# A two-layer encoder trunk: the first weight sums of the second MLP matrices, formed by GpSimd

## The chip, the core and the metric

One core of a Trainium2 chip runs the whole program. Its engines work in parallel, each through its own queue in order: TensorE multiplies, VectorE, ScalarE and GpSimd do element-wise work, SyncE (SP) issues most of the DMAs; GpSimd issues the DMAs that add into on-chip memory. The metric is the device time of one execution in microseconds (us); lower is better.

## The reference

A mixer layer with causal forgetting attention and a second one with chunked attention, each followed by a squared-ReLU MLP, on 256 tokens of width 2048 in float32. The change touches only the MLPs:

```python
D_MODEL = 2048; SEQ = 256; DEPTH = 2; D_FF = 4 * D_MODEL

def rms_norm(x, g):
    xf = x.astype(jnp.float32)
    y = xf * lax.rsqrt(jnp.mean(xf * xf, axis=-1, keepdims=True) + EPS)
    return (y * g.astype(jnp.float32)).astype(x.dtype)

def sq_relu_mlp(h, g, w1, w2):
    a = jax.nn.relu(rms_norm(h, g) @ w1)
    return (a * a) @ w2
...
        h = h + sq_relu_mlp(h, mlp_norm_g[layer], mlp_w1[layer], mlp_w2[layer])
```

## The kernel before

**Products.** The activations stay on the chip as the stationary operand; the weights stream through TensorE once, 512 columns at a time, for two blocks of 128 tokens. To keep float32 accuracy on a faster matmul type, every operand is split into a rounded part `hi` and a remainder `lo`, and each product takes three passes: hi x hi (line 491), lo of the activations x hi of the weights (493), hi x lo of the weights (495). For every weight tile ScalarE makes `hi` (line 227) and VectorE makes `lo`, a subtraction of two on-chip tiles (line 228). There are three `hi` and three `lo` buffers, filled ahead of TensorE by `top_up`.

**Pairs.** In the MLPs two 512-column output panels form a pair. Part of each pair is computed with seven products instead of eight block products (a Strassen-like scheme): the weight blocks are "11", "12", "21", "22", and the products take the tiles "11", T3 = 22 + 12, T2 = T3 + 11, T1 = 12 + 11, "21", T4 = 21 + T2 and "22", in this order (class `Form`). The rest of the pair's weights goes through as plain units of 128 x 1024 (`raw`). An MLP works in four chunks of 2048 hidden columns; each chunk has two pairs for its part of the first matrix and then two for the second matrix. The pairs of the second matrix are "deep" (`p.deep`): their blocks are 2048 columns wide and their forms are used in two halves of 1024 columns. There are 4 x 2 deep pairs in a layer, 16 in all. Below, the first and the second pair mean the two deep pairs of one chunk.

**Who makes the sums.** T3 and T2 are additions in `make` (line 848), T2 in the place of T3 (the tile is named `wT`); T1 and T4 are made by `put` (line 854), a DMA from GpSimd's queue that adds a block from memory to a tile on the chip: T1 to block "12" once T3 has read it, T4 to T2 once T2's `hi` and `lo` are made. `prepare(p, d)` starts the loads of the blocks (`bring`, line 832, SP's queue) and the sums when `d` plain units are left before the pair begins: for the second pair "12" at 7, "22" at 5, "21" at 1, "11" at 4, T3's first half at 3 and its second at 2, T1 at 2; for the first pair "12" at 8, "22" at 6, T3 at 4 and 3.

**Around them.** VectorE also makes `act` (line 882, the low part of the hidden activations), the activation sums of the scheme (lines 296 to 299, and their low part, line 306), transposes finished hidden panels from the accumulators into `z` (line 341), which go through DRAM (lines 351, 357) or directly (`hop`, line 367, eight of its DMAs from GpSimd's queue) to their turned place, and adds finished panels to the residual stream (line 613). The queues of VectorE, ScalarE, TensorE and SP run in the order in which the code is written (`keep_order`); GpSimd is not in that list.

Of the kernel before, what the change touches and what calls it, by code (L numbers as in the profile page):

```python
# [12 lines left out]
ALU = mybir.AluOpType  # L13
# [37 lines left out]
def trunk(ctx: ExitStack, tc: tile.TileContext, xT, xr, gs, hg, bf, wgate, w_in, w_oa, w1a, w1fa, w1sa, w2fa, w2sa,  # L51
          w_kv, w_qb, w_ob, w1b, w1fb, w1sb, w2fb, w2sb, rel, out):
    nc = tc.nc
    V, S, G, TE, SY = nc.vector, nc.scalar, nc.gpsimd, nc.tensor, nc.sync
# [158 lines left out]
    def issue(parts=1):  # L213
        form = None
        if not raws:
            load(parts)
        raw, cuts = raws.popleft()
        if not cuts:
            form, half = raw, raw.half
            raw, cuts = form.pair.t[form.name], [slice(0, form.pair.cols - UN if half else UN)]  # L220
            if half:
                raw = raw[:, UN:]
        n = cuts[-1].stop
        hi = wsp.tile([P, n], F32R, name="hi" if n == UN else "hih", bufs=3 if n == UN else 1)
        lo = wsp.tile([P, n], F32R, name="lo" if n == UN else "loh", bufs=3 if n == UN else 1)
        for c in cuts:
            S.activation(hi[:, c], raw[:, c], AF.Copy)  # L227
            V.tensor_tensor(lo[:, c], raw[:, c], hi[:, c].bitcast(F32), op=ALU.subtract)  # L228
        ready.append((hi, lo, n < UN))
        if form and form.pair.deep and form.name == "T3":  # L230
            make(form.pair, "T2", int(half))
        elif form and half == form.pair.wide:
            if form.name == "T3":
                make(form.pair, "T2")
            elif form.name == "T2" and form.pair.adds:
                put(form.pair, "T4")
# [72 lines left out]
    def room(tag, name, dtype=F32):  # L309
        return qkv.tile([P, DEEP], dtype, name=name, tag=tag, bufs=1)  # L310
# [18 lines left out]
    def steps(make):  # L329
        box = []  # L330

        def step():
            if not box:
                box.append(make())
            next(box[0])
        return step
# [40 lines left out]
    def query_room(i):  # L377

        if not query:
            query.append(prob.tile([P, 4 * UN], F32, name="query", tag="p", bufs=1))  # L380
        return query[0][:, i * UN : i * UN + UN]
# [452 lines left out]
    def make(p, name, half=None):  # L834
        t = p.t
        if half == 1:
            pass
        elif name == "T3":
            if p.order in ("query", ""):
                t[name] = query_room(0)  # L840
            else:
                t[name] = prob.tile([P, 4 * UN], F32, name="wT3", tag="p", bufs=1) if p.order == "early" else room("bias", "wT3")
        else:
            t[name] = t[{"T1": "12", "T2": "T3", "T4": "11"}[name]]
        a, b = {"T1": ("12", "11"), "T3": ("22", "12"), "T2": ("T3", "11"), "T4": ("21", "T2")}[name]
        cols = slice(0, p.cols) if half is None else slice(half * UN, min(half * UN + UN, p.cols))
        d, a, b = (t[i][:, cols] for i in (name, a, b))
        V.tensor_tensor(d, a, b, op=ALU.add)  # L848

    def put(p, name):  # L850

# [262 lines left out]
```

## Time and profile before

| | us |
|---|---|
| median of 3 runs | 2094.65 |
| lowest, highest | 2094.32, 2102.31 |
| span of the profiled execution | 2090.4 |
| TensorE busy | 2076.3 |
| VectorE busy | 1679.5 |
| ScalarE busy | 1288.4 |
| GpSimd busy | 150.1 |

The profile is one execution; its span runs from the first to the last instruction on the engines, and no time of its own stands beside it other than that span. Rows of a timeline read: start, duration, engine, line, operation, output<-inputs, and in brackets the idle time of the engine before it with what ended it. "x2" means two instructions merged into one row. In a group's row, the numbers behind the bar are busy time in us and the mean of one in ns, then the idle time before.

### The profile page before, as it was taken

Reading aid. Unit: us, or ns where it says so; the run is one execution under the profiler, and the core shown is the slowest. Engines: PE = TensorE matmul, PEld = TensorE weight load, DVE = VectorE, ACT = ScalarE, POOL = GpSimd, SP = SyncE. Lnnn points to the kernel's source line nnn. Section 1 sums busy time; section 2 is a strip of 40 time slices with the busy share of each in tenths; the row PEclk is TensorE's granted clock in tenths of the full one; section 3 lists DMA queues with packets and bytes.
Section 4 is the critical chain, followed back from the end, with each engine's and each line's share of the span. In section 5 each row is a group of like instructions: output and inputs, shape, how many; then the busy total and the mean of one; then the engine's idle time right before and its main releaser. Section 6 shows DMA issues by size and latency. Waiting matters only on the chain.

```text
span 2090.4 us, 26489 instructions
## 1 busy us (share of the span) xinstructions
PE 2076.3 (99%) x9182; PEld 1709.6 (82%) x9182; DVE 1679.5 (80%) x1972; ACT 1288.4 (62%) x1613; POOL 150.1 (7%) x195
## 2 busy tenths in 40 slices
PE   9999999999999999999999999999999999999999
PEld 7888888878887887887878888888788788878877
DVE  5767666889789889889988577778988897898886
ACT  6544454767567667667776445556765675676674
POOL 1111000001001001001011001000010010010010
PEclk9999999999999999999999999999999999999999
DMA  7777778789689789788878777787987986897885
GB/s 285 248 253 240 232 255 264 250 268 296 232 292 283 241 270 298 231 273 287 280 252 269 233 232 234 247 264 266 294 280 233 284 284 232 291 286 237 274 279 182
DMA packets 176151, 545.14 MB, mean 261 GB/s; under 512 B 37760, under 2 KB 70416, under 8 KB 163728
## 3 DMA queue, kind: packets, MB, share of 16 engines
q1 hardware_dynamic: 163088, 477.31, 64.4%
q0 software_dynamic: 12640, 65.57, 16.2%
q8 instruction: 72, 1.18, 0.2%
q14 instruction: 63, 0.52, 0.1%
q10 hardware_dynamic: 288, 0.57, 0.1%
HBM read 503.49 MB, written 35.68 MB: 258 GB/s over the span
## 4 chain that ended last, share of the span: by engine, by line
PE 86%; DVE 5%; DMA 5%; ACT 2%; issue 2%; SPq 1%; ACTq 0%; DVEq 0%
PE acc L491 22%; PE acc L493 22%; PE acc L495 22%; PE s L495 6%; PE s L491 5%; PE s L493 5%; DVE lo L228 3%; DMA turn<-z 2%; DMA raw<-in_w1sa 1%; ACT hi L227 1%; PE s L635 1%; PE po L665 1%; DVE z L341 1%; DMA raw<-in_w1sb 1%; SPq L357 0%
## 5 line engine op out<-in xcount | busy, mean ns | idle before, releaser
L228 DVE TENSOR_TENSOR lo<-raw,hi 128x1024 fp32r<-128x1024 f32 (+1 forms) x542 | 655.2, 1214 | 189.3 <-ACT hi L227 176.1
L227 ACT ACTIVATE hi<-raw 128x1024 fp32r<-128x1024 f32 (+1 forms) x542 | 569.3, 1053 | 311.3 <-PE acc L493 232.4
L491 PE MATMUL acc<-hi,act 128*128 128x512 f32 x2092 | 580.4, 394 | 1.3 <-ACT hi L227 1.3
L495 PE MATMUL acc<-lo,act 128*128 128x512 f32 x2092 | 571.6, 390 | 0.0
L493 PE MATMUL acc<-hi,act 128*128 128x512 f32 x2092 | 571.0, 389 | 0.1
L493 PEld LDWEIGHTS acc<-hi,act 128*128 128x128 f32 x2092 | 392.7, 188 | 83.0 <-DVE act L321 0.7
L495 PEld LDWEIGHTS acc<-lo,act 128*128 128x128 f32 x2092 | 391.3, 188 | 84.6 <-DVE lo L228 3.4
L491 PEld LDWEIGHTS acc<-hi,act 128*128 128x128 f32 x2092 | 390.5, 188 | 82.0 <-ACT hi L227 3.2
L227 ACT ACTIVATE hi<-w 128x1024 fp32r<-128x1024 f32 x202 | 212.7, 1057 | 93.4 <-PE acc L493 42.9
L228 DVE TENSOR_TENSOR lo<-w,hi 128x1024 fp32r<-128x1024 f32 x202 | 245.5, 1219 | 22.4 <-ACT hi L227 19.1
L228 DVE TENSOR_TENSOR lo<-wT,hi 128x1024 fp32r<-128x1024 f32 x142 | 172.2, 1221 | 60.8 <-ACT hi L227 59.1
L227 ACT ACTIVATE hi<-wT 128x1024 fp32r<-128x1024 f32 x142 | 148.1, 1055 | 74.4 <-PE acc L493 32.2
L495 PE MATMUL s<-lo,act 128*128 128x512 f32 x370 | 102.1, 392 | 6.0 <-DVE lo L228 6.0
L491 PE MATMUL s<-hi,act 128*128 128x512 f32 x370 | 101.1, 390 | 0.0
L493 PE MATMUL s<-hi,act 128*128 128x512 f32 x370 | 100.9, 389 | 0.0
L495 PEld LDWEIGHTS s<-lo,act 128*128 128x128 f32 x370 | 68.7, 188 | 23.8 <-DVE lo L228 10.1
L493 PEld LDWEIGHTS s<-hi,act 128*128 128x128 f32 x370 | 69.5, 188 | 14.4
L491 PEld LDWEIGHTS s<-hi,act 128*128 128x128 f32 x370 | 69.3, 188 | 14.5 <-ACT hi L227 0.3
L848 DVE TENSOR_TENSOR wT<-wT,w 128x1024 f32<-128x1024 f32 (+1 forms) x48 | 66.3, 1381 | 1.6
L668 ACT ACTIVATE act<-po 128x256 fp32r<-128x256 f32 x32 | 12.3, 385 | 88.0 <-PE po L666 88.0
L848 DVE TENSOR_TENSOR wT<-w,w 128x1024 f32<-128x1024 f32 (+1 forms) x48 | 65.5, 1364 | 0.3 <-DMA w<-in_w2fa 0.3
L577 POOL TENSOR_TENSOR ss<-ss,mhalf 128x4 f32<-128x4 f32 x32 | 43.5, 1367 | 271.8 <-DVE ss L576 271.8
(209 smaller groups left out, 1968.8 us busy)
## 6 DMA issues: line engine op xcount, KB each, us to landing
raw<-in_w_in SPq DMA_DIRECT2D x95, 512.0 KB, 4.6
raw<-in_w1sa SPq DMA_DIRECT2D x70, 512.0 KB, 6.4
raw<-in_w1sb SPq DMA_DIRECT2D x70, 512.0 KB, 6.1
w<-in_w2fa SPq DMA_DIRECT2D x32, 1024.0 KB, 7.7
raw<-in_w2sa SPq DMA_DIRECT2D x64, 512.0 KB, 8.0
raw<-in_w_kv SPq DMA_DIRECT2D x64, 512.0 KB, 4.7
w<-in_w2fb SPq DMA_DIRECT2D x32, 1024.0 KB, 7.5
raw<-in_w2sb SPq DMA_DIRECT2D x64, 512.0 KB, 7.3
```

What stands on the lines that cost most here:

```text
L227: S.activation(hi[:, c], raw[:, c], AF.Copy)
L228: V.tensor_tensor(lo[:, c], raw[:, c], hi[:, c].bitcast(F32), op=ALU.subtract)
L341: V.transpose(z.rearrange("p (j n b c) -> p b n j c", j=4, n=n, b=nb)[:, b], src.rearrange("p (n j c) -> p n j c", n=n, j=4))
L491: TE.matmul(ps[:, cols], xh, cut(hi, j), start=first, stop=False, **kw)
L493: TE.matmul(ps[:, cols], xl, cut(hi, j), start=False, stop=False, **kw)
L495: TE.matmul(ps[:, cols], xh, cut(lo, j), start=False, stop=last, **kw)
L577: G.tensor_tensor(rn, vv, mhalf, op=ALU.pow)
L635: TE.matmul(s[:, P : 3 * P], q[:, a, P:T], k[:, a], start=True, stop=True)
L665: TE.matmul(po[:, :T], v[:, 0, a * P : (a + 1) * P], pT[:, :2], start=True, stop=False)
L668: S.activation(o[i][:, 0], po[:, :T], AF.Copy)
L848: V.tensor_tensor(d, a, b, op=ALU.add)
```

## The change

One line of `make`: in the deep pairs T3's two additions are issued on GpSimd (`G`) instead of VectorE (`V`). T2, and T3 of all other pairs, stay on VectorE.

```diff
         a, b = {"T1": ("12", "11"), "T3": ("22", "12"), "T2": ("T3", "11"), "T4": ("21", "T2")}[name]
         cols = slice(0, p.cols) if half is None else slice(half * UN, min(half * UN + UN, p.cols))
         d, a, b = (t[i][:, cols] for i in (name, a, b))
-        V.tensor_tensor(d, a, b, op=ALU.add)
+        (G if p.deep and name == "T3" else V).tensor_tensor(d, a, b, op=ALU.add)
```

VectorE's queue at a first pair of layer 2 (`wT_15437` is T3, `w_15352` block "22", `w_15270` block "12", `w_15435` block "11"):

```order
 L306 TENSOR_TENSOR Sh<-sum,Sh 128x512 x2
-L848 TENSOR_TENSOR wT_15437<-w_15352,w_15270 128x1024
-L228 TENSOR_TENSOR lo<-raw,hi 128x1024
-L882 TENSOR_TENSOR act<-q,act 128x1024
-L341 STREAM_TRANSPOSE z<-acc 128x4x4x32 x2
-L848 TENSOR_TENSOR wT_15437<-w_15352,w_15270 128x1024
+L228 TENSOR_TENSOR lo<-raw,hi 128x1024
+L882 TENSOR_TENSOR act<-q,act 128x1024
+L341 STREAM_TRANSPOSE z<-acc 128x4x4x32 x2
 L228 TENSOR_TENSOR lo<-w_15435,hi 128x1024
 L296 TENSOR_TENSOR sum<-q 128x256
```

The two additions leave the queue; what stood between and behind them keeps its order.

VectorE's queue at the second pair of the same chunk (`wT_15793` is its T3, `w_15748` its block "11"):

```order
 L228 TENSOR_TENSOR lo<-w_15352,hi 128x1024 x2
 L882 TENSOR_TENSOR act<-q,act 128x1024
-L848 TENSOR_TENSOR wT_15793<-w_15708,w_15605 128x1024
-L228 TENSOR_TENSOR lo<-raw,hi 128x1024 x2
-L228 TENSOR_TENSOR lo<-w_15748,hi 128x1024
-L848 TENSOR_TENSOR wT_15793<-w_15708,w_15605 128x1024
-L228 TENSOR_TENSOR lo<-w_15748,hi 128x1024
+L228 TENSOR_TENSOR lo<-raw,hi 128x1024 x2
+L228 TENSOR_TENSOR lo<-w_15748,hi 128x1024 x2
 L613 SCALAR_TENSOR_TENSOR h_90<-acc,qn,h_90 128x512
```

Here five `lo`, `act` and residual instructions close up where the two additions stood.

GpSimd's queue over both pairs (`w_15270` and `w_15605` become T1, `wT_15437` and `wT_15793` become T4 in the DMAs of line 854):

```order
 L854 DMA w_14968<-in_w1fb 128x1536
 L854 DMA wT_15099<-in_w1fb 128x1536
+L848 TENSOR_TENSOR wT_15437<-w_15352,w_15270 128x1024 x2
 L854 DMA w_15270<-in_w2fb 128x2048
 L854 DMA wT_15437<-in_w2fb 128x2048
 L367 DMA q<-z 32x256 x8
+L848 TENSOR_TENSOR wT_15793<-w_15708,w_15605 128x1024 x2
 L854 DMA w_15605<-in_w2fb 128x2048
 L854 DMA wT_15793<-in_w2fb 128x2048
```

The two additions of a pair stand next to each other, ahead of the pair's T1 and behind the DMAs of the pair before; those of the second pair also stand behind the eight DMAs of the hop.

## The prediction

> **What bounds the kernel now.** I read the page's busy table first, then who waited for whom on TensorE, then the stretches around the moved additions, and last the timelines of VectorE and TensorE there.
>
> ```profile
> span 2090.4 us, 26489 instructions
> PE 2076.3 (99%) x9182; PEld 1709.6 (82%) x9182; DVE 1679.5 (80%) x1972; ACT 1288.4 (62%) x1613; POOL 150.1 (7%) x195
> L495 PE MATMUL s<-lo,act 128*128 128x512 f32 x370 | 102.1, 392 | 6.0 <-DVE lo L228 6.0
> ```
> ```profile
> PEld s L495 <- DVE lo L228: 15.3, 19, 1.4
> PE s L495 <- DVE lo L228: 7.0, 10, 0.9
> ```
> ```profile
> 1819.00:1852.00 33.00, 32.40 (x139) 25.29 (x138) 30.55 (x35) 24.23 (x27) 4.03 (x7) 1.00 0.96 300
> 1852.00:1880.00 28.00, 28.00 (x125) 23.17 (x125) 25.28 (x24) 18.35 (x19) 2.57 (x5) 1.00 0.88 280
> ```
>
> TensorE (PE) is the bound. It is unoccupied for 2090.4 - 2076.3 = 14.1 us in all, and 7.0 us of that are ten waits of line 495, the pass that needs `lo` from VectorE (DVE); the weight loads show 19 such waits. A matmul is drawn 392 ns long, but four of them start in 0.91 us (1867.01 to 1867.92, quoted below), 0.227 us each, so every wait also hides up to 392 - 227 = 0.165 us. All that VectorE's lateness costs TensorE is therefore at most 7.0 + 19 x 0.165 = 10.1 us, 0.48%. No relief of VectorE can bring more. The two stretches are one first and one second pair of the second matrices (columns: length, then PE, PEld, DVE, ACT, POOL busy, clock, DMA share, GB/s). VectorE is busy 30.55 of 33 us and 25.28 of 28 us there: it has some 2.5 us to spare in each, and added VectorE time beyond that must reach TensorE.
>
> **The change, part by part.** It removes 32 additions from VectorE (16 pairs, two each).
>
> ```profile
> L848 DVE TENSOR_TENSOR wT<-w,w x48: 1181/1219/1752, 349.5 to 2035.3; 128x1024 f32<-128x1024 f32 x34, 128x1536 f32<-128x1536 f32 x14
> ```
>
> One takes 1.22 us, but back to back two start 1.14 us apart (1864.32 and 1865.45 below), so a pair gives VectorE 2 x 1.14 = 2.28 us of slots, 36.5 us in all.
>
> It adds two GpSimd (POOL) additions per pair. The trace has no such instruction; the nearest rows are its masks over one input and its small two-input powers, with the VectorE rows beside one power:
>
> ```profile
> L805 POOL TENSOR_SCALAR_AFFINE_SELECT nb<-nb 128x512 f32<-128x512 f32 x4 | 2.5, 634 | 0.0
> masks.py:199 POOL TENSOR_SCALAR_AFFINE_SELECT ident<-ident 128x128 f32<-128x128 f32 x1 | 0.3, 285 | 0.1
> L577 POOL TENSOR_TENSOR ss<-ss,mhalf x32: 1003/1114/1932, 48.0 to 1304.2; 128x4 f32<-128x4 f32 x32
> 1106.04 1.93 POOL L577 TENSOR_TENSOR ss<-ss,mhalf 128x4 f32<-128x4 f32 x1 [9.36 <-DVE ss L576]
> ```
> ```profile
> 1105.85 1.22 DVE L228 TENSOR_TENSOR lo<-query,hi 128x1024 fp32r<-128x1024 f32 x1
> 1106.99 1.22 DVE L228 TENSOR_TENSOR lo<-raw,hi 128x1024 fp32r<-128x1024 f32 x1
> ```
>
> Duration: a mask costs 634 ns for 512 columns and 285 ns for 128, that is 0.91 ns a column and 0.17 us fixed. If 1024 columns of two inputs ran like 1024 of one, the add takes 0.17 + 0.93 = 1.1 us: the lower end. If the inputs are read one after the other, 2048 columns: 0.17 + 1.86 = 2.03 us, or 4 x 634 ns = 2.54 us without splitting off the fixed part: the upper end. I take 2.3 us, between the last two, since the instruction has two inputs.
>
> By the Trainium skill, GPSIMD Engine Reference, section 3.1 (Elementwise — side-by-side cycle accounting), a GpSimd add of two 2048-column inputs takes 4497 ns; half of it, 2.25 us, is an estimate that would move the sum below by less than 2 us.
>
> Contention: a power takes 1.00 us at its shortest. The one at 1106.04 began while a subtraction of two on-chip inputs ran on VectorE (until 1105.85 + 1.22 = 1107.07) and took 1.93 us: 1.03 us of waiting and 0.90 us of work. So a GpSimd read waits for a VectorE instruction with two on-chip inputs, and is let in behind one instruction although the next already stood at 1106.99. Whether VectorE waits the other way round no row shows, as four columns are read in no time. The bounds: VectorE is not held at all, or for the whole 2.3 us. I take the whole, because a read path that makes one side wait for a full instruction is not divided column by column. Every `lo` subtraction (L228), `act` (L882), sum and second weight sum (L848) has two on-chip inputs; the transposes (L341) and the residual updates (L613), which read accumulators, have not.
>
> The Trainium skill, SBUF — State Buffer, section "Who interferes with whom", says just this: a VectorE instruction with two SBUF inputs contends with a GpSimd instruction that reads SBUF, and the later one fully blocks. The trace agrees for the one direction, with the 1.93 us; by that rule the sum is the one below.
>
> Place: on VectorE the second addition had a slot several instructions behind the first; on GpSimd they stand next to each other and start when block 22 has landed. No other operation stands in GpSimd's queue between the previous pair's DMA and them. T1's accumulating DMA behind them had to wait for both additions before, too, so it is not put behind anything new. First pair, layer 2:
>
> ```profile
> 1813.75 0.37 SPq L832 DMA_DIRECT2D w<-in_w2fb  x1
> 1818.28 0.42 SPq L832 DMA_DIRECT2D w<-in_w2fb  x1
> ```
> ```profile
> 1818.93 1.28 DVE L306 TENSOR_TENSOR Sh<-sum,Sh 128x512 fp32r<-128x512 f32 x2
> 1820.13 1.22 DVE L848 TENSOR_TENSOR wT<-w,w 128x1024 f32<-128x1024 f32 x1
> 1821.52 1.23 DVE L228 TENSOR_TENSOR lo<-raw,hi 128x1024 fp32r<-128x1024 f32 x1 [0.17 <-ACT hi L227]
> 1823.56 1.23 DVE L882 TENSOR_TENSOR act<-q,act 128x1024 fp32r<-128x1024 f32 x1 [0.81 <-ACT q L878]
> 1824.70 1.31 DVE L341 STREAM_TRANSPOSE z<-acc 128x512 f32<-128x512 f32 x2
> 1825.93 1.18 DVE L848 TENSOR_TENSOR wT<-w,w 128x1024 f32<-128x1024 f32 x1
> 1827.09 1.23 DVE L228 TENSOR_TENSOR lo<-w,hi 128x1024 fp32r<-128x1024 f32 x1
> 1829.70 1.22 DVE L228 TENSOR_TENSOR lo<-w,hi 128x1024 fp32r<-128x1024 f32 x1
> ```
> ```profile
> 1829.00 0.62 PE L495 MATMUL s<-lo,act 128*128 128x512 f32 x2
> 1830.97 0.73 PE L495 MATMUL s<-lo,act 128*128 128x512 f32 x2 [0.45 <-DVE lo L228]
> ```
>
> Block 22 was issued at 1813.75 and used at 1820.13 without a wait, so it was there by then; I let the first add start after the first half of L306, 1819.6 to 1821.9. L306's other half follows (to 1822.4), then the second add (to 1824.7), then `lo` 1824.7, L882 1825.9, the transposes 1827.0 to 1828.3. The `lo` of 1827.09 thus starts at 1828.3, ends at 1829.5, 0.5 us after TensorE wanted it (1829.00). The sums and the next `lo`, 2.61 us behind it in the rows, start 1.06 us later than 1829.70 once the last slack is used; at 1830.97 TensorE already stands waiting, so the whole 1.06 us is new: **+1.06 us per first pair**.
>
> Second pair, layer 2:
>
> ```profile
> 1863.17 1.23 DVE L882 TENSOR_TENSOR act<-q,act 128x1024 fp32r<-128x1024 f32 x1 [0.82 <-ACT q L878]
> 1864.32 1.22 DVE L848 TENSOR_TENSOR wT<-w,w 128x1024 f32<-128x1024 f32 x1
> 1865.45 2.35 DVE L228 TENSOR_TENSOR lo<-raw,hi 128x1024 fp32r<-128x1024 f32 x2
> 1868.86 1.22 DVE L848 TENSOR_TENSOR wT<-w,w 128x1024 f32<-128x1024 f32 x1
> 1869.99 1.22 DVE L228 TENSOR_TENSOR lo<-w,hi 128x1024 fp32r<-128x1024 f32 x1
> ```
> ```profile
> 1867.01 1.07 PE L495 MATMUL acc<-lo,act 128*128 128x512 f32 x4
> 1867.92 1.07 PE L491 MATMUL acc<-hi,act 128*128 128x512 f32 x4
> 1869.73 1.07 PE L495 MATMUL acc<-lo,act 128*128 128x512 f32 x4
> ```
>
> Add one 1864.3 to 1866.6, the first `lo` 1866.6 to 1867.8 (wanted at 1867.01: 0.8 us late), add two 1867.7 to 1870.0, the second `lo` 1870.0 to 1871.3 (wanted at 1869.73): **+1.6 us per second pair**. From there on the freed slot at 1868.86 brings VectorE back and nothing more is lost.
>
> Sum: 8 x 1.06 + 8 x 1.6 = 8.5 + 12.8 = **+21 us**. Against the profiled span 2090.4 us that is 2111.7; the median of the runs, 2094.65, lies 4.25 us above the span, and gives **2116 us**. With 1.8 us per add the same steps leave nothing at the first pairs and about 0.6 us at the second, +5 us; with 2.54 us, 1.5 and 2.1, +29 us.
>
> **Rivals.** (1) No blocking, or adds short enough to fit VectorE's spare time: not slower than before. For it: VectorE's rows show no held instruction anywhere; against it: the 1.93 us power. Little would be gained even so. The stalls of the first pairs begin at `lo` 1827.09, whose `hi` waits not for VectorE but for a weight block:
>
> ```profile
> 1826.00 2.01 ACT L227 ACTIVATE hi<-w 128x1024 fp32r<-128x1024 f32 x2 [2.47 <-DVE z L341]
> w<-in_w2fb SPq DMA_DIRECT2D x32, 1024.0 KB, 7.5
> ```
>
> The row names the transpose, but `hi` reads nothing of it; block 11, issued at 1818.28, lands a median 7.5 us later, at 1825.8. The removed addition leaves a hole there. I give this 2094 us. (2) The two adds hold the path as one, without letting VectorE in between: the first pair is unchanged in sum, but at the second the first `lo` starts at 1864.3 + 4.6 = 1868.9 and ends at 1870.1, 3.1 us after 1867.01: 8.5 + 8 x 3.1 = +33 us, 2128 us. For it: the adds are neighbours in the queue; against it: the power was let in behind one instruction, so turns are taken. (3) The freed slots remove all of VectorE's stalls: at best -10.1 us, 2085 us; against it, the weight block above.
>
> **How the numbers follow.** The forecast has 0.55, rival 1 0.23, rival 2 0.15, rival 3 0.07. A measurement here tells about 0.5% from no change, 10.5 us: below 2084.2 faster, above 2105.1 slower. Even rival 3 at its best stays inside; faster gets 0.03 for what I have not seen. Slower is nearly all of the forecast (short adds near 1.9 us fall inside) and rival 2, 0.67; the same 0.30. The forecast's own range is 2100 to 2124; with rival 1 below and rival 2 above, 2092 to 2132.
>
> **What would show it.** GpSimd adds of 2.0 to 2.6 us, or longer when they wait; a `lo` or `act` row beside them that starts or ends about 2.3 us late, or is itself drawn longer; more idle before L495, released by `lo` of L228, at both kinds of pair, from 7 us to some 25 us; an unchanged matmul spacing of 0.227 us. `lo` rows that run at 1.22 us while an add runs would show rival 1. A forecast much too low would mean that z, late by 2.3 us at 1827.0, also delays its turn through DRAM and the loads behind it on the SP queue.

## The result

| | us |
|---|---|
| before, median of the runs beside the changed kernel | 2096.53 (2094.32 to 2102.31) |
| changed, median of 4 runs | 2123.78 (2123.11 to 2124.84) |
| ratio | 1.0132, 95% interval 1.0113 to 1.0151 |
| span of the profiled execution, before and changed | 2090.4 and 2121.3 |

The change costs 1.3%, some 27 us in the medians and 30.9 us between the two profiled spans. In every run on record the time lies 1.7 to 2.1 us above the span, so the profiled execution before, with its span of 2090.4 us, was a quick one; that is most of the difference between 27 and 30.9. The forecast was slower, 2116 us, range 2092 to 2132.

From the page of the changed kernel, its busy times and two of its groups of instructions:

```profile
span 2121.3 us, 26508 instructions
PE 2087.3 (98%) x9182; PEld 1709.1 (81%) x9182; DVE 1695.1 (80%) x1940; ACT 1287.5 (61%) x1613; POOL 243.7 (11%) x227
...
L228 DVE TENSOR_TENSOR lo<-raw,hi 128x1024 fp32r<-128x1024 f32 (+1 forms) x542 | 674.6, 1250 | 193.2 <-ACT hi L227 180.7
L848 POOL TENSOR_TENSOR wT<-w,w 128x1024 f32<-128x1024 f32 x32 | 94.1, 2957 | 219.3 <-DMA w<-in_w2fa 78.2
```

VectorE lost 32 instructions and is busy 15.6 us longer than before: 1695.1 against 1679.5. E4 below has the same remaining instructions with nothing held, and its VectorE is busy 1643.1 us; the change thus draws them longer by 52 us in all. Who waited for whom on TensorE, in the changed kernel (us in total, times, the longest):

```profile
PE acc L495 <- DVE lo L228: 12.2, 6, 2.1
PE s L495 <- DVE lo L228: 9.6, 12, 0.9
PE acc L493 <- DVE act L882: 3.2, 3, 1.7
```

TensorE's waits for VectorE rise from 7.0 to 25.0 us; the waits at `acc` and for `act` are new. By the busy rows TensorE is unoccupied for 34.0 us instead of 14.1, and for the same matmuls it is busy 11.0 us longer, in part for the reason told in the last section. The first pair of layer 2 that the prediction followed, on VectorE, GpSimd and TensorE:

```profile
1841.48 3.50 DVE L306 TENSOR_TENSOR Sh<-sum,Sh 128x512 fp32r<-128x512 f32 x2
1844.90 3.43 DVE L228 TENSOR_TENSOR lo<-raw,hi 128x1024 fp32r<-128x1024 f32 x1
1848.25 1.21 DVE L882 TENSOR_TENSOR act<-q,act 128x1024 fp32r<-128x1024 f32 x1
1849.39 1.30 DVE L341 STREAM_TRANSPOSE z<-acc 128x512 f32<-128x512 f32 x2
1850.62 1.17 DVE L228 TENSOR_TENSOR lo<-w,hi 128x1024 fp32r<-128x1024 f32 x1
```
```profile
1841.63 5.62 POOL L848 TENSOR_TENSOR wT<-w,w 128x1024 f32<-128x1024 f32 x2 [20.90 <-DVE lo L228]
```
```profile
1851.85 0.73 PE L495 MATMUL s<-lo,act 128*128 128x512 f32 x2
1854.45 0.73 PE L495 MATMUL s<-lo,act 128*128 128x512 f32 x2 [0.94 <-DVE lo L228]
```

L306's two halves took 1.28 us before and take 3.50 now: the second half stood 2.2 us. The `lo` at 1844.90 takes 3.43 us instead of 1.23, again 2.2 us. The two additions lie over these two instructions. The wait at 1854.45 is 0.94 us where before it was 0.45.

### The profile page after: what moved, and what is told of

The parts are those of the page before. It is cut to its first block, busy times and chain, and to the rows that moved or that the text cites. A ratio compares the mean times of both kernels' runs of the same rounds, so it can differ in the third digit from the quotient of the medians.

```text
span 2121.3 us, 26508 instructions
## 1 busy us (share of the span) xinstructions
PE 2087.3 (98%) x9182; PEld 1709.1 (81%) x9182; DVE 1695.1 (80%) x1940; ACT 1287.5 (61%) x1613; POOL 243.7 (11%) x227
## 4 chain that ended last, share of the span: by engine, by line
PE 75%; DMA 11%; DVE 6%; issue 3%; ACT 2%; SPq 1%; POOL 0%; ACTq 0%; DVEq 0%; POOLq 0%
PE acc L495 21%; PE acc L493 20%; PE acc L491 20%; PE s L495 4%; PE s L491 4%; PE s L493 4%; DVE lo L228 3%; DMA turn<-z 3%; DMA raw<-in_w2sa 3%; DMA w<-in_w2fb 1%; DMA q<-turn 1%; ACT hi L227 1%; DMA raw<-in_w2sb 1%; DVE z L341 1%; DVE act L882 1%
## 5 line engine op out<-in xcount | busy, mean ns | idle before, releaser
L228 DVE TENSOR_TENSOR lo<-raw,hi 128x1024 fp32r<-128x1024 f32 (+1 forms) x542 | 674.6, 1250 | 193.2 <-ACT hi L227 180.7
L848 POOL TENSOR_TENSOR wT<-w,w 128x1024 f32<-128x1024 f32 x32 | 94.1, 2957 | 219.3 <-DMA w<-in_w2fa 78.2
```

Source lines behind the costliest of these rows:

```text
L848: (G if p.deep and name == "T3" else V).tensor_tensor(d, a, b, op=ALU.add)
```

## The experiments

**E1 and E2: one kind of pair at a time.** `p.units[0]` is 8 in the first pairs and 7 in the second ones.

```diff
-        V.tensor_tensor(d, a, b, op=ALU.add)
+        (G if p.deep and name == "T3" and p.units[0] == 8 else V).tensor_tensor(d, a, b, op=ALU.add)
```

The second pairs alone have 7 in the place of 8. Expected of the first pairs:

> T3's additions on GpSimd in the first pairs alone (16 additions); the second pairs as before. Theory (a GpSimd addition and a two-input VectorE instruction shut each other out of the on-chip memory's read path): the first pairs' share of the loss, +1.06 us each by the prediction, 8 to 9 us in all, about 2104 us, and no stretch of TensorE's clock below 1.00. Rival (the loss comes from GpSimd's queue and T1's DMA behind the additions, which is the same in every pair): half of the whole loss, +13 to +15 us.

Expected of the second pairs:

> T3's additions on GpSimd in the second pairs alone (16 additions). Theory: the second pairs' share, about +2.2 us each and 1.7 us more wherever the stall lets TensorE's clock fall to half for 3.4 us: +18 us without such falls, +23 to +25 us with three or four, about 2114 to 2121 us. Rival (GpSimd's queue and T1's DMA): half of the whole loss, +13 to +15 us.

Measured: first pairs 2101.82 us against 2094.62, ratio 1.0037 (1.0021 to 1.0052), +7.2 us; second pairs 2112.28 us, 1.0093 (1.0075 to 1.0112), +17.7 us. The first pairs cost a little less than the expected 8 to 9 us; the second pairs end just below their expected range, and neither shows the rival's 13 to 15 us. The same operations in the same queue cost more than twice as much at the second pairs, so it is not a fixed price of GpSimd's queue or of T1's DMA. TensorE's waits with the second pairs alone:

```profile
PE acc L493 <- DVE act L882: 7.8, 6, 1.6
PE s L495 <- DVE lo L228: 7.2, 9, 1.0
PE acc L495 <- DVE lo L228: 3.8, 2, 1.9
```

The middle row is about what the kernel before has (7.0); the waits at `acc`, for `act` and for `lo`, are what the second pairs add.

**E3: GpSimd as busy, without reading.** T3's sums give way to one added column and three times zeros.

```diff
+        if p.deep and name == "T3":
+            G.tensor_tensor(d[:, :1], a[:, :1], b[:, :1], op=ALU.add)
+            for _ in range(3):
+                G.memset(d[:, 1:], 0.0)
+            return
         V.tensor_tensor(d, a, b, op=ALU.add)
```

> GpSimd adds only the first column of each half of T3 and then writes zeros three times over the other columns, some 2.5 us of work as long as the addition was; so the sums of T3 are left out of the result. VectorE has lost the 32 additions, as in the changed kernel, and GpSimd is as busy, but reads next to nothing. Theory (the read path is what is shared): no subtraction drawn longer than 1.3 us, time between 2084 and 2097 us. Rival 1 (any GpSimd work beside VectorE, or sums that come from another engine's semaphore, costs the same): 2115 to 2125 us.

Measured: 2107.13 us, 1.0063 (1.0048 to 1.0078). Half of the expectation held and half did not. No subtraction is drawn longer: zeros were being written during 63 `lo` and 16 `act`, none of which is drawn longer than 1.23 us, and the group of `lo` has a mean of 1213 ns, 1214 before:

```profile
L228 DVE TENSOR_TENSOR lo<-raw,hi 128x1024 fp32r<-128x1024 f32 (+1 forms) x542 | 654.7, 1213 | 204.9 <-ACT hi L227 193.4
```

But the time is 12.5 us over before, by a wait that neither theory had:

```profile
PE s L491 <- ACT hi L227: 13.2, 8, 2.6
```

At a first pair, on SP's queue, GpSimd and ScalarE (lines of this kernel; 851 is the zeros, 849 the one added column, 859 the accumulating DMA of `put`):

```profile
1832.83 0.42 SPq L832 DMA_DIRECT2D w<-in_w2fb  x1
```
```profile
1824.53 4.54 POOL L851 MEMSET wT<- 128x1023 f32 x5
1833.63 1.19 POOL L849 TENSOR_TENSOR wT<-w,w 128x1 f32<-128x1 f32 x2 [4.56 <-DMA w<-in_w2fb]
1835.22 0.85 POOL L859 DMA_DIRECT2D w<-in_w2fb  x1 [0.41 <-POOL wT L849]
```
```profile
1843.01 2.01 ACT L227 ACTIVATE hi<-w 128x1024 fp32r<-128x1024 f32 x2 [4.82 <-DMA w<-in_w2fb]
```

The zeros do not need block 22, and GpSimd writes them before it lands. Only the two one-column sums then stand between its landing and T1's DMA. So this DMA, which adds 1 MB to block 12, is issued 2.4 us after block 11's load instead of 9.2 us as before (1818.28 and 1827.52). Block 11 is then used 10.2 us after its issue; before, it was used 7.7 us after (1818.28 to 1826.00). That fits the eight waits for `hi`. It also means that the zeros are not written at the moments at which the changed kernel adds.

**E4 and E10: the same two kernels with that transfer out of the way.** In the first pairs block 11 is loaded one unit earlier. E4 is E3 with this line, E10 the changed kernel with it; their code differs only in what GpSimd does for T3.

```diff
-                add(None, w2f, w2s, i, WIDE2, "deep", close if q else (8,6,1,4,4,2), DEEP)
+                add(None, w2f, w2s, i, WIDE2, "deep", close if q else (8,6,1,5,4,2), DEEP)
```

> As the kernel with zeros written, and the load of weight block 11 issued one unit earlier in the first pairs; T3's sums are left out again. Theory (with VectorE relieved, the stalls of the first pairs are held by the landing of block 11): 3 to 9 us faster than the kernel with zeros alone, the ten waits of line 495 of some 7 us mostly gone. Rival (the stalls are held by VectorE's sums behind): no difference within 2 us.

> The changed kernel with only the load of block 11 issued one unit earlier in the first pairs, as in the kernel of 2090.15 us whose GpSimd wrote zeros; the two differ in what GpSimd reads. Theory (GpSimd's two reads shut VectorE's two-input instructions out for the length of the addition): 20 to 30 us slower than that kernel, 2110 to 2121 us, with subtractions drawn up to 3.4 us long. Rival (the loss of the changed kernel is a matter of when T1's DMA and block 11's load are on the way, which this load order mends): within 5 us of 2090.

Measured: E4 2090.15 us, 0.9979 (0.997 to 0.9989), 17 us below E3, more than the expected 3 to 9; its waits of line 495 at `s`, expected to be mostly gone, are still seven with 4.4 us. E10 2127.92 us, 1.0156 (1.0138 to 1.0174), above its expected range: its profiled execution has six falls of TensorE's clock in the second pairs (last section), with a mean granted clock of 0.994. With one load order, 38 us lie between additions that read 2048 columns and zeros that read next to none, although GpSimd is as busy (246.8 us in E10, 248.8 in E4). Together with the rows of held instructions beside the additions, and none beside the zeros, this shows the reads as the cause. E4 also says what freeing VectorE of these sums brings with this load order if nothing is paid: 4.5 us.

**E7 and E11: the same additions in smaller pieces.** Four instructions of 256 columns (E7) or two of 512 (E11) for each one of 1024.

```diff
+        if p.deep and name == "T3":
+            for c in (slice(i * 256, i * 256 + 256) for i in range(4)):
+                G.tensor_tensor(d[:, c], a[:, c], b[:, c], op=ALU.add)
+            return
         V.tensor_tensor(d, a, b, op=ALU.add)
```

> As the changed kernel, but each addition of 1024 columns is made as four of 256 columns, all on GpSimd. Theory (the path is held for one instruction, and the other side goes next): no subtraction is drawn longer than about 2.1 us, no single wait of line 495 above 1.6 us, TensorE's clock stays at 1.00, but the added VectorE time is the same or larger, so 2105 to 2118 us, faster than the changed kernel by 5 to 15 us. Rival (the path is shared column by column, and only the number of columns counts): the same time as the changed kernel within 4 us.

> As the changed kernel, with each addition of 1024 columns made as two of 512, on GpSimd: the size between the changed kernel (1024 columns, 29 us slower than before) and that of 256 columns (no difference). Theory (what counts is how late VectorE is at any one moment, set by the length of one hold, against 1 to 2.5 us of slack; not the sum of the holds, which is about the same in all three): holds of 1.1 to 1.3 us, no `lo` drawn longer than 2.6 us, stalls of some 0.5 to 1 us per pair and no fall of TensorE's clock, 2098 to 2110 us. Rival (the sum of the holds counts, and 256 columns are cheap because a short addition holds the path for a smaller part of its time): additions of 512 columns lie on the line by columns, within 4 us of 2094.8 + 2/3 of 29 us, 2110 to 2118 us.

| columns in one addition | us | ratio | interval |
|---|---|---|---|
| 1024 (the change) | 2123.78 | 1.0132 | 1.0113 to 1.0151 |
| 512 (E11) | 2100.88 | 1.0034 | 1.0021 to 1.0048 |
| 256 (E7) | 2094.83 | 0.9999 | 0.9988 to 1.001 |

E7 fell out of its expected range on the good side: the loss is gone altogether, although its range rested on VectorE being held as long in sum. E11 lies in the theory's range and not in the rival's. The additions on GpSimd by line (shortest, median, longest in ns), of E7 and of E11:

```profile
L850 POOL TENSOR_TENSOR wT<-w,w x128: 725/1459/1808, 449.8 to 2039.6; 128x256 f32<-128x256 f32 x128
```
```profile
L850 POOL TENSOR_TENSOR wT<-w,w x64: 1280/2267/2296, 449.1 to 2041.4; 128x512 f32<-128x512 f32 x64
```

A second pair of layer 2 in E7, VectorE and GpSimd (886 is `act` here):

```profile
2032.43 1.56 DVE L886 TENSOR_TENSOR act<-q,act 128x1024 fp32r<-128x1024 f32 x1 [0.81 <-ACT q L882]
2033.92 3.44 DVE L228 TENSOR_TENSOR lo<-raw,hi 128x1024 fp32r<-128x1024 f32 x2
2037.28 3.43 DVE L228 TENSOR_TENSOR lo<-w,hi 128x1024 fp32r<-128x1024 f32 x2
```
```profile
2029.79 11.53 POOL L850 TENSOR_TENSOR wT<-w,w 128x256 f32<-128x256 f32 x8 [5.55 <-DVE lo L228]
```

Two `lo` take 3.44 us instead of 2.35, 0.55 us more each: one short addition before each of them. How long VectorE is held in sum follows from its busy time, against the 1643.1 us of E4. These are the busy rows of E4, E11 and E7:

```profile
PE 2077.7 (99%) x9182; PEld 1708.6 (82%) x9182; DVE 1643.1 (79%) x1940; ACT 1287.1 (62%) x1613; POOL 248.8 (12%) x323
PE 2080.5 (99%) x9182; PEld 1706.8 (81%) x9182; DVE 1690.2 (80%) x1940; ACT 1288.0 (61%) x1613; POOL 275.2 (13%) x259
PE 2077.2 (99%) x9182; PEld 1707.3 (82%) x9182; DVE 1672.9 (80%) x1940; ACT 1287.9 (62%) x1613; POOL 308.6 (15%) x323
```

The holds sum to 52 us with 1024 columns (1695.1), 47 us with 512 and 30 us with 256. So the theory's premise, about the same sum in all three, holds for 1024 and 512 only. Between these two the sum falls by a tenth and the loss from 27 to 6 us: what counts there is the length of one hold. The changed kernel pays up to 4.4 us within two instructions. E7 spreads smaller holds over 7.6 to 12 us a pair, and is also held less in sum; its runs do not tell the two apart.

**E9 and E8: a schedule for VectorE instead.** Both of T3's additions at one place in the first pairs, on VectorE; E9 with block 11 as before, E8 with block 11 one unit earlier as well.

```diff
-        if p.deep and d == p.units[4] - 1:
+        if p.deep and p.units[0] == 7 and d == p.units[4] - 1:
             make(p, "T3", 1)
...
                 make(p, "T3", 0)
+                if p.units[0] == 8:
+                    make(p, "T3", 1)
```

> The kernel before, with the second addition of T3 in the first pairs made right after the first, still on VectorE; T1's DMA can then start some 4 us after block 11's load instead of 9 us. Theory (what is bought on VectorE is given back where T1's DMA runs beside block 11's load): block 11 lands 1 to 2.5 us later after its issue than before (7.7 us), and the time is 2 to 12 us slower than before. Rival (VectorE's place alone counts): 0 to 9 us faster than before.

> The kernel before, with both additions of T3 in the first pairs made together on VectorE, as in the last kernel, and block 11's load issued one unit earlier. Theory: neither VectorE nor block 11 holds the first pairs' stalls any more, 4 to 10 us faster than before, 2085 to 2091 us. Rival (the activation sums behind hold the stalls): within 2 us of before.

Measured: E9 2096.43 us, 1.0007 (0.9997 to 1.0017); E8 2095.17 us, 1.0001 (0.9992 to 1.0011). Neither expectation of the theory held. E9's time lies outside its rival's range too; E8's lies in its rival's, but the rival's reason, the activation sums, was not tested. In E9 T1's DMA starts 4.6 us after block 11's load in most pairs, and block 11 is about as early as before: the disturbance of E3 needs transfers closer together than that. In E8 the waits that were to go are gone:

```profile
PE acc L495 <- DVE lo L228: 1.5, 4, 0.5
...
PE s L495 <- DVE lo L228: 0.9, 1, 0.9
```

and the time is the same. Comparing the start of the same matmul in the two traces, E8 wins some 4 us in the first pairs and loses as much behind them. The row of waits at `acc` above is new, and so is most of ScalarE's wait for the turned hidden panel that comes back from DRAM; before and E8:

```profile
ACT q L871 <- DMA q<-turn: 0.4, 2, 0.2
```
```profile
ACT q L873 <- DMA q<-turn: 5.1, 6, 1.8
```

Behind its longest wait of this kind, 1.8 us, TensorE loses 1.7 us. Why the panel comes later was not tried.

**E12: short additions and the early load.** A version meant to beat both kernels: E7 with E4's load order.

> Additions of 256 columns on GpSimd in all deep pairs and block 11's load one unit earlier in the first pairs: a version meant to beat both kernels, since with the same load order and no reads by GpSimd the time was 2090.15 us. Theory (VectorE relieved, short holds, block 11 there in time): 2 to 7 us faster than before, 2088 to 2093 us. Rival (the holds take back what the freed slots bring at the first pairs): within 2 us of before or slower.

Measured: 2102.56 us, 1.0041 (1.0028 to 1.0053), slower than E7 and than before. At a first pair of layer 2:

```profile
1825.36 9.52 POOL L850 TENSOR_TENSOR wT<-w,w 128x256 f32<-128x256 f32 x8 [21.14 <-DMA w<-in_w2fb]
```
```profile
1833.32 0.95 DVE L296 TENSOR_TENSOR sum<-q 128x256 f32<-128x256 f32 x1
1834.31 0.85 DVE L297 TENSOR_TENSOR sum<-q,sum 128x256 f32<-128x256 f32 x1
```

The activation sums are drawn 0.95 and 0.85 us instead of 0.42: the additions now reach into them. But TensorE's wait behind them is no longer than E7's at this pair (0.94 us); its time is lost 11 us later. TensorE, then ScalarE, of E12:

```profile
1837.02 0.74 PE L495 MATMUL s<-lo,act 128*128 128x512 f32 x2 [0.46 <-DVE lo L228]
1848.34 0.73 PE L491 MATMUL s<-hi,Sh 128*128 128x512 f32 x2 [0.46 <-ACT hi L227]
```
```profile
1846.28 1.06 ACT L875 ACTIVATE q<-q 128x1024 f32<-128x1024 f32 x1 [1.41 <-DMA q<-turn]
1847.24 1.04 ACT L227 ACTIVATE hi<-wT 128x1024 fp32r<-128x1024 f32 x1
```

ScalarE waits for the turned hidden panel, and `hi` behind it in its queue comes late. E12 has 11.6 us of these waits in all, E7 3.3 us; between the two profiled spans lie 5.9 us. So the rival's number came out, and its reason is not shown. What makes the panel late, the early load or the DMA of T1 that here starts within half a microsecond of the panel's, was not tried. No version here beats the kernel before by what can be told apart, except E4, which leaves sums out.

## Why the prediction was right, and where its size was off

**The bound and the sign.** TensorE was the bound and had at most 10.1 us to win. The relieved VectorE with the early load (E4) brought 4.5 us. The forecast of slower rested on the read path, and E10 against E4 shows it.

**The duration.** 2.3 us was taken for one addition; the shortest is drawn 2.39 us (E1: 2385 ns) and the holds on VectorE are 2.2 us. The end of 2.54 us was too long, 1.1 us far too short.

**Whole blocking, in turns.** The trace before had it in one direction only. The changed kernel shows the other one, 3.43 us instead of 1.23, and that VectorE goes in between the two additions: L306 is held by one and `lo` by the other. Rival 2, both additions as one hold, falls by these rows, although its sum for the second pairs (8 x 3.1 = 25 us) was nearer the measured one. By the Trainium skill, SBUF — State Buffer, section "Who interferes with whom", the side that issues second fully blocks until the first is done; these rows agree, now in both directions.

**The sum by pairs.** From the starts of the same matmul in the two profiled executions:

| | predicted, us | measured, us |
|---|---|---|
| 8 first pairs | +8.5 | +8.8 |
| 8 second pairs, up to the next first pair | +12.8 | +23.7 |
| program start | 0 | -1.5 |
| sum | +21 | +30.9 |

The cuts between the pairs move the first two sums by some 0.4 us. The first pairs came out as worked in sum, in part by luck: each lost 0.4 to 2.1 us, and the held rows are the predicted ones, half of L306 and then `lo`, in three of the eight (the followed pair of layer 2 is one), while in three others a single `act` is held. The step that was mis-sized is the term "+1.6 us per second pair": 3.0 us in the mean. Two things made it so. The place: I let the first addition begin where T3 had stood on VectorE, behind `act`. It begins when block 22 has landed, as the prediction itself said, and that is earlier: in all 16 pairs within 0.2 us of the landing, which in the second pairs comes some 5 to 6 us after the issue and not the median 7.5 us of all these loads. The second pair of the last chunk in the changed kernel, where block 22 landed at 2054.67 (the bracket of the addition names a `lo` that ended a little earlier):

```profile
2054.61 1.23 DVE L228 TENSOR_TENSOR lo<-w,hi 128x1024 fp32r<-128x1024 f32 x1 [0.74 <-ACT hi L227]
2056.66 2.54 DVE L882 TENSOR_TENSOR act<-q,act 128x1024 fp32r<-128x1024 f32 x1 [0.82 <-ACT q L878]
2059.12 4.52 DVE L228 TENSOR_TENSOR lo<-raw,hi 128x1024 fp32r<-128x1024 f32 x2
```
```profile
2054.80 6.62 POOL L848 TENSOR_TENSOR wT<-w,w 128x1024 f32<-128x1024 f32 x2 [5.97 <-DVE lo L228]
```
```profile
2059.25 1.21 PE L493 MATMUL acc<-hi,act 128*128 128x512 f32 x4 [0.16 <-DVE act L882]
2062.56 1.56 PE L495 MATMUL acc<-lo,act 128*128 128x512 f32 x4 [2.10 <-DVE lo L228]
2063.92 1.91 PE L491 MATMUL acc<-hi,act 128*128 128x512 f32 x4
```

The first addition holds `act` (2.54 us for 1.23), so the second holds the first `lo`, not the second one as I had it. That `lo` has next to no slack, and TensorE stands 2.1 us. So it went in six of the eight second pairs; in the other two, the followed one of layer 2 among them, the first addition holds a `lo` and the second `act`. The other thing is what the prediction put at nothing, an unchanged matmul spacing of 0.227 us: behind that stall four matmuls take 1.7 us from start to start (2063.92 to about 2065.63) where four take 0.91 otherwise. TensorE's clock had dropped; this is in the last section.

**The last step of the sum.** The forecast put 4.25 us between span and time. The runs have 1.7 to 2.1 us there; the rest was the quick profiled execution before.

**The rivals.** Rival 1 (no blocking) falls by E10. Its side argument, that block 11's landing holds the first pairs as well, was right as far as it went: in the changed kernel the row of `hi` names that load,

```profile
1848.79 2.01 ACT L227 ACTIVATE hi<-w 128x1024 fp32r<-128x1024 f32 x2 [2.83 <-DMA w<-in_w2fb]
```

but E8 shows that mending it gains nothing by itself. Rival 3 had its bound of 10.1 us; E4 reached less than half of it. The price "+5 us with 1.8 us per add, +29 us with 2.54" already had the loss grow faster than the addition, since it went by lateness against slack; E11 against the change shows the same, with a tenth less held in sum and less than a quarter of the loss.

## What to carry to other kernels

An addition moved to an idle GpSimd is not off VectorE if both read two on-chip tiles: count up to its full duration as VectorE time (here 1.6 of at least 2.4 us in the mean, 52 us over 32 additions), at the moment its data lands, against the slack of the instruction that stands there. If such work must run on GpSimd, cut it into short instructions, so that VectorE gets in between them: here 1024, 512 and 256 columns cost 27, 6 and 0 us for the same sums. An instruction that leaves a queue also moves the DMA that waited for it; look for the load that is then on the way.

## What the runs showed of the hardware

TensorE's clock falls after short stalls. Three stretches of the changed kernel around a stall of 1.9 us (columns: length, then PE, PEld, DVE, ACT, POOL busy with counts, the granted clock, DMA share, GB/s):

```profile
1718.00:1721.70 3.70, 1.79 (x9) 1.17 (x8) 3.70 (x3) 1.12 (x2) 3.29 (x2) 1.00 0.21 82
1721.75:1725.10 3.35, 3.35 (x9) 2.62 (x9) 3.12 (x3) 0.86 (x1) 0.00 (x0) 0.51 0.90 150
1725.20:1728.00 2.80, 2.80 (x13) 2.25 (x12) 1.38 (x3) 1.06 (x1) 0.00 (x0) 0.99 1.02 238
```

The clock is 0.51 for 3.35 us after the stall and 0.99 again behind it: 8 matmuls start there, 0.43 us apart, where 15 would have (3.35 / 0.227), some 1.6 us more. It happened at three of the eight second pairs, some 5 of their 23.7 us, each time behind a stall in which two matmuls started 2.3 to 2.5 us apart; three other stalls of that length in the same execution had no such fall, and no shorter one had. The record of the clock dates the falls at 670.54, 1721.84 and 2063.18 us and each lasts 3.41 us; the distances are 308.0 and 100.0 times 3.413 us. In a grid of such steps the three stalls with a fall lie inside one step, and the three without cross from one step to the next. E10 also has falls behind stalls that cross, so this is not the whole rule. The Trainium skill, TensorE: Matmul & The Clock Gate, section "Why this matters for your kernels", asks for no gaps above about 3 us; here an idle time of 1.9 us, with starts 2.3 us apart, sufficed at times.

An accumulating DMA of 1 MB issued 2.4 us behind a load of 1 MB goes with a use 10.2 us after that load's issue instead of 7.7 us (E3); at 4.6 us (E9) this was not seen. In E3's eight first pairs the load landed 9.8 to 10.8 us after its issue, before 7.3 to 8.6 us.
